# The last MLP's first product as seven block products, in two passes over the features

## The chip, the core and the metric

The kernel runs on one core of one Trainium2 chip. The metric is the device time of one execution in microseconds (us), the median of several runs. The core has five engines with a queue each: TensorE (PE in the profile, its weight loads listed apart as PEld), VectorE (DVE), ScalarE (ACT), GpSimd (POOL) and SyncE (SP), which here issues most of the DMAs. Each engine takes the instructions of its queue in order; between engines they wait on semaphores.

## What is computed

A two-layer encoder trunk for 256 + 1024 = 1280 tokens of 1024 features. Each layer has a mixer and an MLP. The part that matters is the MLP of the second layer, the last step of the kernel:

```python
h = rms_norm(x, norm_mlp[layer, 0])
f = jnp.einsum('bld,df->blf', h, w_ff_in[layer])
f = jnp.einsum('blf,fd->bld', jnp.square(jax.nn.relu(f)), w_ff_out[layer])
x = x + rms_norm(f, norm_mlp[layer, 1])
```

`w_ff_in` is 1024 x 4096, `w_ff_out` 4096 x 1024, all in float32.

## The kernel before

**Products.** A float32 product is made of three matmuls on values split in a high part and a low part: `mm3` (L249 to L256) multiplies high by high, high by low and low by high. `split` (L243 to L247) makes the two parts: a cast on ScalarE (L246) and a subtraction on VectorE (L247). A matmul takes 128 x 128 weights and up to 512 columns of tokens.

**Tokens and features.** The tokens are ten tiles of 128, in two halves of 640 (HT). The 4096 hidden features (DFF) are 32 tiles of 128, or NP = 16 pairs j. The 1024 input features are KT = 8 tiles.

**First product** (`mlp`, from L338; called for the last MLP at L2094). For a feature tile f the weights come in as 512 KB (`w1load`, `raw` in the profile), are split into `w` (three buffers), and then 24 matmuls each (8 tiles k times 3) go over 512 and 256 columns of `xT1` and 512 columns of `xT0`, into PSUM tiles `psi`. `xT0` holds four token tiles that `mixer_out`, the step ahead, has normed and transposed; the other six tiles are normed (`pre_a`) and transposed (`pre_b`, eight transposes into a PSUM tile `pst`, then copies to `xT1`) inside this stage while six feature tiles go over the `xT0` columns ahead. The PSUM pool of `psi` and `pst` has three double banks.

**Between the products.** Each result goes through Relu (L386) and Square (L387) on ScalarE into a staging tile `st`. A pair of feature tiles and two token halves make four blocks of 128 x 640; `sums` (L368 to L376) makes three more by four additions on VectorE, and `store` (L380 to L382) writes all seven, 2240 KB, to DRAM as `hd[j]`.

**Second product** (L436 to the end of `mlp`). It uses seven block products already: with the blocks of `hd[j]` (loads `hr`, split into `hs`) and sums of blocks of `w_ff_out`, seven steps i over 16 pairs k, results in PSUM tiles `po` (L512). 

**What sets the order.** Engines run in program order as the code is written, save that a scheduler may move instructions on a queue when the program is built. SP's queue holds the weight loads, the stores of `hd` and the loads of `hr` in one line. The buffers of the pools, reused in turn, set when a load may start.

Of the kernel before, what the change touches and what calls it, by code (L numbers as in the profile page):

```python
# [13 lines left out]
ALU = mybir.AluOpType  # L14
# [39 lines left out]
def drain(g):  # L54
    for _ in g:
        pass
# [126 lines left out]
class Trunk:  # L183
# [151 lines left out]

    def mlp(self, layer, lay, xT0, g1, side=(), tail=None):  # L338


        side = iter(side)
# [2 lines left out]
        w1, w2 = I["w_ff_in"][layer], I["w_ff_out"][layer]  # L344
        NP = DFF // 256
        with ExitStack() as c:

            cf = ExitStack()
            sp = self.pool(cf, "st", 2, side="right")
            xT1 = self.pool(cf, "xT1", 1, side="right").tile([128, 2, KT, 768], F32R, name="xT1")  # L350
            cx = c.enter_context(ExitStack())
            self.xp = self.pool(cx, "x", 2)
            self.hbp = self.pool(cx, "hb", 2)
            tts = [self.halves[0][4], *self.halves[1]]
            hb = {}

            def norm(i):
                hb[i] = self.pre_a(self.load_x(lay, tts[i]), g1)

            def transpose(i):  # L360
                self.pre_b(hb.pop(i), xT1, (i - 1) % 6 * 128)
            g = pipe(6, norm, lambda i: None, transpose)
            stage = {}

            def w1load(f):
                return self.w8load(w1[:, f * 128:(f + 1) * 128].rearrange("(k p) f -> p k f", p=128), [KT, 128])

            def sums(j):  # L368

                t = stage.pop(j)  # L370
                a11, a21, a12, a22, s1, s2, s4 = (t[:, i] for i in range(7))
                v.tensor_tensor(s1, a21, a22, op=ALU.add)
                v.tensor_tensor(a21, a11, a21, op=ALU.subtract)
                v.tensor_tensor(s2, s1, a11, op=ALU.subtract)
                v.tensor_tensor(s4, a12, s2, op=ALU.subtract)
                stores.append((j, t))  # L376
# [12 lines left out]
            def ffin(f, W, parts):  # L389

                j, z = divmod(f, 2)
                if j not in stage:
                    stage[j] = sp.tile([128, 7, HT], F32, tag="st", name="st")
                d = stage[j][:, 2 * z:2 * z + 2].rearrange("p a t -> p (a t)")
                for o, m, ps in parts:
                    x, i = (xT1, o) if o < 768 else (xT0, o - 768)
                    self.mm3(ps[:, :m], [((W[:, 0, k], W[:, 1, k]), (x[:, 0, k, i:i + m], x[:, 1, k, i:i + m]))
                                         for k in range(KT)])
                    act(ps[:, :m], d[:, o:o + m])

            def banks():
                b = self.bank2([128, 2, 512], "psi")
                return b[:, 0], b[:, 1]

            AHEAD = 6
            jobs = [(f, 0) for f in range(AHEAD)] + [(f, 1) for f in range(AHEAD)] + [(f, None) for f in range(AHEAD, 2 * NP)]
            next(g)
            next(g)
            W = w1load(0)
            odd = None  # L410
            for n, (f, h) in enumerate(jobs):
                parts = []
                if h != 0:
                    b = banks()
                    parts += [(0, 512, b[0]), (512, 256, b[1])]
                if h != 1:
                    if f % 2 == 0:
                        odd = banks()
                    parts.append((768, 512, odd[f % 2]))
                ffin(f, W, parts)  # L420
                if n + 1 < len(jobs):
                    W = w1load(jobs[n + 1][0])
                if h == 0:
                    next(g, None)
                    if f == AHEAD - 1:
                        cx.close()
                        self.cg.close()
                    continue
                if stores:
                    store()  # L430
                if f % 2:
                    sums(f // 2)
                for _ in range(7 if h else 12):
                    next(side, None)
            drain(side)
            cf.close()  # L436
            hp = self.pool(c, "hr", 4)

            ap = [self.pool(c, "am0", 1)]
# [133 lines left out]

            def next2(t):
                self.pre_b(hb.pop(t), nx[0], (t + 4) % 5 * 128)
            sq = {}

            def half(t):
# [45 lines left out]
    class OutProj:  # L624
# [37 lines left out]
        def product(self, i):  # L662
            self.partial(i, self.order)
            del self.M[i]
# [1287 lines left out]
        self.xp = self.pool(c, "x", 2)  # L1952
        self.hbp = self.pool(c, "hb", 2)

    def mixer_out(self, op, layer, head=0):


        I = self.I
        self.gp = self.g1p
        g1 = self.load_gain(I["norm_mlp"][layer, 0:1, :])  # L1960
        xT = self.xtp.tile([128, 2, KT, 512], F32R, tag="xT", name="xT")
        hb = {}
        with ExitStack() as c:
            self.xp = self.pool(c, "x", 2)
# [25 lines left out]

            def finish(i):
                y = op.finish(i, g)
                if i < 4:
                    hb[i] = self.pre_a(y, g1)

            def transpose(i):
                if i < 4:
                    self.pre_b(hb.pop(i), xT, i * 128)

            def product(i):  # L2000
# [7 lines left out]
    def run(self):  # L2008
# [117 lines left out]
```

## Time and profile before

| what | value |
|---|---|
| median of 3 runs | 3134.39 us (3132.23 to 3135.25) |
| the profiled execution, its own time | 3131.81 us |
| its span | 3130.0 us |
| its mean granted TensorE clock | 0.991 |
| TensorE busy | 3031.6 us, 97% of the span |
| weight loads / VectorE / ScalarE / GpSimd busy | 84% / 64% / 40% / 11% |
| DMA | 507.37 MB, mean 162 GB/s |

The span is the time between the first and the last instruction of one execution as the profiler saw it. Times in the rows below are microseconds from the start of that span, unless they are marked as ns. The granted clock is the share of full speed that TensorE was given; 1.00 is 2.4 GHz and 0.50 is 1.2 GHz. The first product of the last MLP runs from about 2282 to 2738 us.

### The profile page before, as it was taken

Reading aid. Unit: us, or ns where it says so; the run is one execution under the profiler, and the core shown is the slowest. Engines: PE = TensorE matmul, PEld = TensorE weight load, DVE = VectorE, ACT = ScalarE, POOL = GpSimd, SP = SyncE. Lnnn points to the kernel's source line nnn. Section 1 sums busy time; section 2 is a strip of 40 time slices with the busy share of each in tenths; the row PEclk is TensorE's granted clock in tenths of the full one; section 3 lists DMA queues with packets and bytes.
Section 4 is the critical chain, followed back from the end, with each engine's and each line's share of the span. In section 5 each row is a group of like instructions: output and inputs, shape, how many; then the busy total and the mean of one; then the engine's idle time right before and its main releaser. Section 6 shows DMA issues by size and latency. Waiting matters only on the chain. (4 is left out here: it accounts for less than half of the span.)

```text
span 3130.0 us, 44212 instructions
## 1 busy us (share of the span) xinstructions
PE 3031.6 (97%) x16768; PEld 2627.5 (84%) x16768; DVE 1998.1 (64%) x3678; ACT 1258.2 (40%) x2269; POOL 329.9 (11%) x555
## 2 busy tenths in 40 slices
PE   8999989999999999999999999997999999999998
PEld 7878878788888788888999899996888888888887
DVE  6688865667767665676865499998542212165765
ACT  5577763444444333354223221112343222243343
POOL 1045640000100000000000223221000000000000
PEclk9999999999999999999999999999999999999999
DMA  4100034456556774676987633324544332464674
GB/s 148 54 13 11 12 104 147 142 187 215 185 168 193 260 225 123 214 229 217 332 312 269 197 116 103 129 86 145 153 149 163 135 133 100 154 218 144 225 233 141
DMA packets 309794, 507.37 MB, mean 162 GB/s; under 512 B 19476, under 2 KB 198646, under 8 KB 297036
## 3 DMA queue, kind: packets, MB, share of 16 engines
q1 hardware_dynamic: 300780, 467.02, 45.5%
q0 software_dynamic: 8800, 37.51, 3.6%
q8 instruction: 132, 2.16, 0.3%
q14 instruction: 82, 0.67, 0.1%
HBM read 340.61 MB, written 163.85 MB: 161 GB/s over the span
## 5 line engine op out<-in xcount | busy, mean ns | idle before, releaser
L255 PE MATMUL psi<-xT,w 128*128 128x512 f32 (+1 forms) x4608 | 915.8, 356 | 6.2 <-DVE xT L247 3.6
L255 PEld LDWEIGHTS psi<-xT,w 128*128 128x128 f32 x4608 | 753.0, 188 | 137.0 <-ACT st L386 14.8
L512 PE MATMUL po<-w,hs 128*128 128x512 f32 x3360 | 777.4, 393 | 4.0 <-ACT hs L246 4.0
L512 PEld LDWEIGHTS po<-w,hs 128*128 128x128 f32 x3360 | 631.6, 189 | 147.6 <-ACT hs L246 4.4
L247 DVE TENSOR_TENSOR w<-raw,w 128x1024 fp32r<-128x1024 f32 (+1 forms) x192 | 182.3, 952 | 351.0 <-ACT w L246 350.7
L247 DVE TENSOR_TENSOR hs<-hr,hs 128x640 fp32r<-128x640 f32 x224 | 183.6, 823 | 239.4 <-ACT hs L246 239.2
L246 ACT CAST hs<-hr 128x640 fp32r<-128x640 f32 x224 | 163.1, 729 | 426.2 <-PE po L512 399.4
L255 PE MATMUL psz<-xT,w 128*128 128x320 f32 (+2 forms) x1920 | 292.2, 311 | 2.6 <-ACT w L246 1.9
L386 ACT ACTIVATE st<-psi 128x512 f32<-128x512 f32 (+1 forms) x192 | 101.0, 526 | 469.8 <-PE psi L255 469.7
L255 PEld LDWEIGHTS psz<-xT,w 128*128 128x128 f32 x1920 | 284.0, 189 | 4.7 <-ACT w L246 2.3
L1048 POOL TENSOR_TENSOR P<-P,sm 128x256 f32<-128x256 f32 x272 | 162.5, 628 | 148.4 <-DVE sm L1045 143.4
L246 ACT CAST w<-raw 128x1024 fp32r<-128x1024 f32 (+1 forms) x192 | 158.9, 829 | 42.4 <-DMA raw<-odd_w_in 13.9
L255 PE MATMUL pso<-wo,M 128*128 128x512 f32 x660 | 159.3, 397 | 8.7 <-ACT M L246 7.1
L255 PEld LDWEIGHTS pso<-wo,M 128*128 128x128 f32 x660 | 124.7, 190 | 38.3 <-ACT M L246 7.3
L1392 PE MATMUL psu<-Z,fb 128*128 128x128 f32 x768 | 100.8, 289 | 19.0 <-DVE t L1731 13.7
L1392 PEld LDWEIGHTS psu<-Z,fb 128*128 128x128 f32 x768 | 95.5, 203 | 23.5 <-issue 16.8
L255 PE MATMUL pss<-kt,qt 128*128 128x512 f32 (+3 forms) x432 | 111.8, 386 | 3.3 <-DVE PT L247 3.0
L387 ACT ACTIVATE st<-st 128x512 f32<-128x512 f32 (+1 forms) x192 | 107.6, 560 | 3.3
L247 DVE TENSOR_TENSOR w<-am,w 128x512 fp32r<-128x512 f32 x128 | 87.0, 684 | 33.3 <-ACT w L246 33.3
L220 POOL DMA_DIRECT2D gain<-norm_mlp x4 | 2.2, 558 | 945.2 <-DVE w L247 926.8
L247 DVE TENSOR_TENSOR PT<-pspt,PT 128x1024 fp32r<-128x1024 f32 (+1 forms) x72 | 83.7, 1163 | 20.0 <-ACT PT L246 19.0
L255 PEld LDWEIGHTS pss<-kt,qt 128*128 128x128 f32 (+1 forms) x432 | 75.6, 189 | 15.9 <-PE pspt L1056 3.6
(341 smaller groups left out, 4160.2 us busy)
## 6 DMA issues: line engine op xcount, KB each, us to landing
hd<-st SPq DMA_DIRECT2D x32, 2240.0 KB
hr<-hd SPq DMA_DIRECT2D x224, 320.0 KB
raw<-w_ff_out SPq DMA_DIRECT2D x112, 512.0 KB
raw<-w_ff_in SPq DMA_DIRECT2D x76, 512.0 KB
x<-xd SPq DMA_DIRECT2D x47, 512.0 KB
wd<-w SPq DMA_DIRECT2D x20, 1024.0 KB
w<-wd POOLq DMA_DIRECT2D x20, 1024.0 KB, 5.4
dec<-c_decay SPq DMA_DIRECT2D x120, 128.0 KB
```

Source lines behind the costliest of these rows:

```text
L220: self.nc.gpsimd.dma_start(g, row.broadcast_to([128, D]))
L246: self.nc.scalar.copy(hi, src)
L247: (eng or self.nc.vector).tensor_tensor(lo, src, hi, op=ALU.subtract)
L255: self.nc.tensor.matmul(out, lhsT=lt[a], rhs=r[b], start=start and i == 0, stop=stop and i == n - 1)
L386: nc.scalar.activation(d, ps, AF.Relu)
L387: nc.scalar.activation(d, d, AF.Square)
L512: nc.tensor.matmul(P[i][t], lhsT=h[:, x, t * 128:(t + 1) * 128], rhs=w[:, y], start=k + n == 0, stop=k == NP - 1 and n == 2)
L1048: nc.gpsimd.tensor_tensor(p, p, sm[:, 2:3].to_broadcast([128, 256]), op=ALU.mult)
L1392: self.nc.tensor.matmul(ps[:, out], lhsT=FB[:, pos, i, out], rhs=z, start=i == 0, stop=i == 1)
```

## The change

The last MLP's first product becomes a product of 2 x 2 blocks as well. The blocks are: input features in two halves of four tiles k, tokens in two halves of 640, the two feature tiles of a pair j. Seven products of 512 x 128 blocks with 512 x 640 blocks take the place of eight. `mlp` gets a flag `blocks`, which is set for the last MLP alone; the first MLP runs the old code, now called `plain`.

Two passes over the 16 pairs:

- Pass 1 makes, for each j, the two products that need no sums of blocks: the weights of the pair's first feature tile by `xT0`, 24 matmuls of 320 columns for each of two column halves, lower four k and upper four k. The first result (p1) is copied from PSUM to `pc`, the second is added to it (`c11`), `c11` goes through Relu and Square, and both, 640 KB, are stored in `hd[j]`. In the same pass the five tiles of the second token half are normed and transposed, and `operands` makes the five right-hand blocks X by six additions and five splits for each tile.
- Pass 2 loads the weights again, as two loads of 512 KB for each j, makes five left-hand operands by four additions and five splits (`wparts`), loads p1 and `c11` back (`prefetch`) and makes the other five products, six additions of 640 columns, three pairs of Relu and Square, and then `sums` and `store` of 2240 KB as before.

`mixer_out` transposes five tiles now (n=5), and `xT0` has 640 columns. The staging tile of pass 2 takes the space of `xT0`. `wslots` moves to a function, and the order of tiles at the end of the MLP is rotated (`rot`).

In the diff lines that are only "..." stand for what is left out; `plain` is the old code, further indented.

```diff
-    def mlp(self, layer, lay, xT0, g1, side=(), tail=None):
+    def mlp(self, layer, lay, xT0, g1, side=(), tail=None, blocks=False):
...
+            def plain():
...
+            def strassen():
+                cf = ExitStack()
+                opp = self.pool(cf, "xo", 1, side="right")
+                X = {q: opp.tile([128, 2, 4, HT], F32R, name=f"xo{q}") for q in (4, 3, 5, 7, 6)}
+                cx = ExitStack()
+                pp = self.pool(cx, "pc", 1)
+                tp = self.pool(cx, "xs", 1)
+                xp = self.pool(cx, "x", 2)
+                xb = {}
+                def norm(i):
+                    x = xb[i] = xp.tile([128, D], F32, tag="x", name="x")
+                    nc.sync.dma_start(x, self.x_src(lay, self.halves[1][i]))
+                    sm = self.small()
+                    self.square_sum(x, sm)
+                    self.root(sm, D)
+                    r = self.rstd(sm, D)
+                    v.scalar_tensor_tensor(x, x, r, g1, op0=ALU.mult, op1=ALU.mult)
+                def operands(i):
+                    x = xb.pop(i)
+                    ps = self.bank2([128, KT, 128], "pst")
+                    for k in range(KT):
+                        nc.tensor.transpose(ps[:, k], x[:, k * 128:(k + 1) * 128], self.ident)
+                    b = tp.tile([128, KT, 128], F32, tag="xb", name="xb")
+                    nc.scalar.copy(b, ps)
+                    b12, b22 = b[:, 0:4], b[:, 4:8]
+                    t = slice(i * 128, (i + 1) * 128)
+                    p = tp.tile([128, 4, 128], F32, tag="xp", name="xp")
+                    q = tp.tile([128, 4, 128], F32, tag="xq", name="xq")
+                    v.tensor_tensor(p, xT0[:, 0, 0:4, t], xT0[:, 1, 0:4, t], op=ALU.add)
+                    v.tensor_tensor(q, b22, b12, op=ALU.subtract)
+                    self.split(X[7][:, :, :, t], q)
+                    v.tensor_tensor(p, b12, p, op=ALU.subtract)
+                    self.split(X[5][:, :, :, t], p)
+                    v.tensor_tensor(q, b22, p, op=ALU.subtract)
+                    self.split(X[6][:, :, :, t], q)
+                    v.tensor_tensor(p, xT0[:, 0, 4:8, t], xT0[:, 1, 4:8, t], op=ALU.add)
+                    self.split(X[3][:, :, :, t], b22)
+                    v.tensor_tensor(p, q, p, op=ALU.subtract)
+                    self.split(X[4][:, :, :, t], p)
+                g = pipe(5, norm, lambda i: None, operands)
+                def product(w, x):
+                    ps = self.bank2([128, 2, 512], "psi")
+                    for c in range(2):
+                        o = slice(c * 320, c * 320 + 320)
+                        self.mm3(ps[:, c, :320], [((w[:, 0, k], w[:, 1, k]), (x[:, 0, k, o], x[:, 1, k, o]))
+                                                  for k in range(4)])
+                    return ps[:, :, :320]
+                def cols(t):
+                    return t.rearrange("p (a t) -> p a t", a=2)
+                next(g)
+                next(g)
+                W = w1load(0)
+                for j in range(NP):
+                    pc = pp.tile([128, 2, HT], F32, tag="pc", name="pc")
+                    p1, c11 = cols(pc[:, 0]), cols(pc[:, 1])
+                    nc.scalar.copy(p1, product(W[:, :, 0:4], xT0[:, :, 0:4]))
+                    ps = product(W[:, :, 4:8], xT0[:, :, 4:8])
+                    if j + 1 < NP:
+                        W = w1load(2 * j + 2)
+                    v.tensor_tensor(c11, p1, ps, op=ALU.add)
+                    act(pc[:, 1], pc[:, 1])
+                    nc.sync.dma_start(self.hd[j][:, 0:2], pc)
+                    if j % 2 == 0:
+                        next(g, None)
+                drain(g)
+                cx.close()
+                self.cg.close()
+                cw = ExitStack()
+                wp = self.pool(cw, "wr", 4)
+                tp = self.pool(cw, "wt", 2)
+                st = self.xtp.tile([128, 2, 7, HT], F32, tag="xT", name="st")
+                ring = wring()
+                raws, parts = {}, []
+                def wload(j):
+                    if j < NP:
+                        raws[j] = [self.raww(w1[z * 512:(z + 1) * 512, j * 256:(j + 1) * 256]
+                                             .rearrange("(k p) f -> p k f", p=128), [4, 256], wp) for z in range(2)]
+                def wparts():
+                    n = 0
+                    for j in range(NP):
+                        lo, hi = raws.pop(j)
+                        a11, a21, a12, a22 = lo[:, :, 0:128], lo[:, :, 128:256], hi[:, :, 0:128], hi[:, :, 128:256]
+                        s3 = tp.tile([128, 4, 128], F32, tag="wt", name="s3")
+                        wload(j + 1)
+                        v.tensor_tensor(s3, a11, a21, op=ALU.subtract)
+                        v.tensor_tensor(a21, a21, a22, op=ALU.add)
+                        v.tensor_tensor(a11, a21, a11, op=ALU.subtract)
+                        for q, src in enumerate((a11, s3, a21, a12, a22)):
+                            if q == 3:
+                                v.tensor_tensor(a12, a12, a11, op=ALU.subtract)
+                            t = ring[n % len(ring)].rearrange("p (a k f) -> p a k f", a=2, k=4)
+                            n += 1
+                            self.split(t, src)
+                            parts.append(t)
+                            yield
+                wgen = wparts()
+                def prefetch(j):
+                    if j < NP:
+                        stage[j] = st[:, j % 2]
+                        nc.sync.dma_start(stage[j][:, 0:2], self.hd[j][:, 0:2])
+                wload(0)
+                prefetch(0)
+                for _ in range(4):
+                    next(wgen)
+                for j in range(NP):
+                    t = stage[j]
+                    u, c22, c21 = cols(t[:, 0]), cols(t[:, 2]), cols(t[:, 3])
+                    for q in (6, 7, 5, 3, 4):
+                        ps = product(parts.pop(0), X[q])
+                        next(wgen, None)
+                        if q == 6:
+                            v.tensor_tensor(u, u, ps, op=ALU.add)
+                            if j:
+                                sums(j - 1)
+                        elif q == 7:
+                            v.tensor_tensor(c21, u, ps, op=ALU.add)
+                        elif q == 5:
+                            v.tensor_tensor(c22, c21, ps, op=ALU.add)
+                            v.tensor_tensor(u, u, ps, op=ALU.add)
+                            act(t[:, 2], t[:, 2])
+                            if j:
+                                store()
+                        elif q == 3:
+                            v.tensor_tensor(u, u, ps, op=ALU.add)
+                            act(t[:, 0], t[:, 0])
+                            prefetch(j + 1)
+                        else:
+                            v.tensor_tensor(c21, c21, ps, op=ALU.subtract)
+                            act(t[:, 3], t[:, 3])
+                sums(NP - 1)
+                cw.close()
+                cf.close()
+            def wring():
+                return [t[:, i * 1024:(i + 1) * 1024] for t in [self.w8.tile([128, 2048], F32R, tag="w8", name="w4")
+                                                                for _ in range(self.nw8)] for i in range(2)]
+            (strassen if blocks else plain)()
...
-            wslots = [t[:, i * 1024:(i + 1) * 1024] for t in [self.w8.tile([128, 2048], F32R, tag="w8", name="w4")
-                                                              for _ in range(self.nw8)] for i in range(2)]
+            wslots = wring()
...
+            rot = 0 if blocks else 4
...
-                tt = self.halves[0][(t + 4) % 5]
+                tt = self.halves[0][(t + rot) % 5]
...
-    def mixer_out(self, op, layer, head=0):
+    def mixer_out(self, op, layer, head=0, n=4):
...
-        xT = self.xtp.tile([128, 2, KT, 512], F32R, tag="xT", name="xT")
+        xT = self.xtp.tile([128, 2, KT, n * 128], F32R, tag="xT", name="xT")
...
-                if i < 4:
+                if i < n:
...
-            xT, g1 = self.mixer_out(op, 1)
+            xT, g1 = self.mixer_out(op, 1, n=5)
...
-            self.mlp(1, 3, xT, g1)
+            self.mlp(1, 3, xT, g1, blocks=True)
```

**The order of instructions.** Three places, as the built programs have them.

ScalarE in the first product, before, one feature tile. `st<-psi` is Relu and `st<-st` Square; `w<-raw` is the high part of the next tile's weights:

```order
L386 ACTIVATE st<-psi 128x512
L246 CAST w<-raw 128x1024
L387 ACTIVATE st<-st 128x512
L386 ACTIVATE st<-psi 128x512
L387 ACTIVATE st<-st 128x512
L386 ACTIVATE st<-psi 128x256
L387 ACTIVATE st<-st 128x256
```

Here the cast of the weights stands among the activations of one tile.

ScalarE in pass 1, after, around the copy of a transposed tile (`xb<-pst`). `xo` are the parts of X, `xq` and `xp` the sums they are made of, `pc<-psi` the copy of p1:

```order
L246 CAST w<-raw 128x1024
L472 COPY xb<-pst 128x1024
L506 COPY pc<-psi 128x640
L246 CAST xo_21062<-xb 128x4x128
L246 CAST xo_21064<-xq 128x4x128
L373 ACTIVATE pc<-pc 128x640
L246 CAST xo_21063<-xp 128x4x128
L374 ACTIVATE pc<-pc 128x640
```

The cast of the weights now stands ahead of the copy that frees the PSUM banks of the transposes, and the copy of p1 behind it.

SP in the first product, before (`hd_111` is `hd[3]`):

```order
L382 DMA hd_111<-st 128x4480
L470 DMA hr<-hd_111 128x640
L260 DMA raw<-w_ff_in 128x8x128 x2
L382 DMA hd_112<-st 128x4480
L470 DMA hr<-hd_112 128x640
L260 DMA raw<-w_ff_in 128x8x128 x2
```

For each pair there are one store, one load for the second product and two weight loads.

SP at the change of passes, after (`hd_108` is `hd[0]`, `hd_123` is `hd[15]`; `raw` of 128x4x256 are weight loads of pass 2):

```order
L512 DMA hd_120<-pc 128x1280
L512 DMA hd_121<-pc 128x1280
L512 DMA hd_122<-pc 128x1280
L555 DMA st<-hd_108 128x1280
L555 DMA st<-hd_109 128x1280
L512 DMA hd_123<-pc 128x1280
L260 DMA raw<-w_ff_in 128x4x256 x8
L369 DMA hd_108<-st 128x4480
L260 DMA raw<-w_ff_in 128x4x256 x2
L555 DMA st<-hd_110 128x1280
```

The loads of half results for the first two pairs have moved ahead of the last store of pass 1, and the first weight loads of pass 2 stand behind it. From then on a round has one store, two weight loads and one load of half results.

## Rows read from the trace of the kernel before

**Rows 1.** The page's chain of work that ended last, by line.

```profile
PE psi L255 14%; PE po L512 12%; PE pso L255 3%; PE psz L255 3%; PE psu L1392 2%; PE pe L1739 1%; PE po L1739 1%; DVE t L1729 0%; PE pe L1741 0%; PE po L1741 0%; POOL Y L1732 0%; PE psu L1838 0%; POOL Y L1733 0%; PE psya L1739 0%; DMA w<-wd 0%
```

**Rows 2.** Windows: us, busy of PE, PEld, DVE, ACT, POOL, PEclk, DMA share, GB/s.

```profile
2324.00:2737.60 413.60, 413.60 (x2161) 350.06 (x2160) 91.69 (x102) 127.72 (x220) 0.00 (x0) 1.00 0.38 136
```

**Rows 3.** Timeline of PE: start, us, engine, line, operation, out<-in, count.

```profile
2281.87 5.65 PE L255 MATMUL psi<-xT,w 128*128 128x512 f32 x24
...
2296.19 5.72 PE L255 MATMUL psi<-xT,w 128*128 128x512 f32 x24
2301.75 1.03 PE L297 MATMUL pst<-ident,hb 128*128 128x128 f32 x8
2302.60 5.76 PE L255 MATMUL psi<-xT,w 128*128 128x512 f32 x24
...
2737.60 22.60 PE L512 MATMUL po<-w,hs 128*128 128x512 f32 x99
```

**Rows 4.** Timeline of PE and PEld in the Hyena input product.

```profile
1545.76 7.15 PEld L255 LDWEIGHTS psz<-xT,w 128*128 128x128 f32 x48
1545.78 7.39 PE L255 MATMUL psz<-xT,w 128*128 128x320 f32 x48
1553.01 1.89 PE L1469 MATMUL pss<-zp,fa 128*128 128x256 f32 x8
```

**Rows 5.** Groups by line and shape, first product: busy, mean ns, idle before.

```profile
L255 PEld LDWEIGHTS psi<-xT,w 128*128 128x128 f32 x2302 | 376.4, 188 | 72.2 <-ACT st L386 7.3 <-DVE xT L247 2.0
L247 DVE TENSOR_TENSOR w<-raw,w 128x1024 fp32r<-128x1024 f32 x35 | 42.9, 1226 | 290.3 <-ACT w L246 290.3
...
L246 ACT CAST w<-raw 128x1024 fp32r<-128x1024 f32 x35 | 36.5, 1042 | 2.9 <-PE psi L255 2.9
...
L372 DVE TENSOR_TENSOR st<-st 128x640 f32<-128x640 f32 x15 | 12.3, 819 | 0.0
...
L246 ACT CAST xT<-pst 128x1024 fp32r<-128x1024 f32 x6 | 6.0, 1011 | 0.0
```

**Rows 6.** Groups by line and shape from 2200 to the end.

```profile
L246 ACT CAST hs<-hr 128x640 fp32r<-128x640 f32 x112 | 81.8, 730 | 217.7 <-PE po L512 202.6 <-issue 10.8 <-DMA hr<-hd 4.1
...
L247 DVE TENSOR_TENSOR w<-am,w 128x512 fp32r<-128x512 f32 x64 | 43.7, 685 | 32.0 <-ACT w L246 32.0
...
L246 ACT CAST w<-am 128x512 fp32r<-128x512 f32 x64 | 39.4, 616 | 0.0
```

**Rows 7.** The tile psz, ScalarE's copy: least, median, greatest ns.

```profile
L1540 ACT COPY zs<-psz x20: 692/692/699, 1477.5 to 1689.3; 128x640 f32<-128x640 f32 x20
```

**Rows 8.** Timeline of SP's DMA issues and of the first reader.

```profile
2241.07 0.37 SPq L260 DMA_DIRECT2D raw<-w_ff_in  x1
...
2245.01 1.05 ACT L246 CAST w<-raw 128x1024 fp32r<-128x1024 f32 x1 [5.28 <-DMA raw<-w_ff_in]
...
2342.26 0.34 SPq L382 DMA_DIRECT2D hd<-st  x1
...
2349.14 0.34 SPq L470 DMA_DIRECT2D hr<-hd  x1
...
2408.71 0.34 SPq L382 DMA_DIRECT2D hd<-st  x1
2417.35 0.34 SPq L470 DMA_DIRECT2D hr<-hd  x1
...
2420.17 0.73 ACT L246 CAST hs<-hr 128x640 fp32r<-128x640 f32 x1 [1.49 <-DMA hr<-hd]
```

**Rows 9.** Timeline of PE around an idle stretch in the mixer.

```profile
2153.97 0.73 PE L255 MATMUL pso<-xT,M 128*128 128x512 f32 x2 [1.33 <-ACT M L246]
2162.42 5.26 PE L255 MATMUL pso<-xT,M 128*128 128x512 f32 x13 [7.73 <-DVE M L247]
2167.52 0.63 PE L255 MATMUL pso<-wo,M 128*128 128x512 f32 x2
```

**Rows 10.** The window behind that stretch, columns as in rows 2.

```profile
2160.00:2165.00 5.00, 2.58 (x6) 2.09 (x7) 5.00 (x14) 1.05 (x1) 0.00 (x0) 0.50 0.55 216
```

More of the change, by code (lines that the diff above doesn't have):

```diff
@@ L346, in mlp @@
         with ExitStack() as c:
[L348 to L362, printed above, removed]
             stage = {}
@@ L387, in act @@
                 nc.scalar.activation(d, d, AF.Square)
[L389 to L434, printed above, removed]
@@ L435, in mlp, with transpose, ffin, banks @@
-            drain(side)
-            cf.close()
+            def plain():
+                cf = ExitStack()
+                sp = self.pool(cf, "st", 2, side="right")
+                xT1 = self.pool(cf, "xT1", 1, side="right").tile([128, 2, KT, 768], F32R, name="xT1")
+                cx = c.enter_context(ExitStack())
+                self.xp = self.pool(cx, "x", 2)
+                self.hbp = self.pool(cx, "hb", 2)
+                tts = [self.halves[0][4], *self.halves[1]]
+                hb = {}
+                def norm(i):
+                    hb[i] = self.pre_a(self.load_x(lay, tts[i]), g1)
+                def transpose(i):
+                    self.pre_b(hb.pop(i), xT1, (i - 1) % 6 * 128)
+                g = pipe(6, norm, lambda i: None, transpose)
+                def ffin(f, W, parts):
+                    j, z = divmod(f, 2)
+                    if j not in stage:
+                        stage[j] = sp.tile([128, 7, HT], F32, tag="st", name="st")
+                    d = stage[j][:, 2 * z:2 * z + 2].rearrange("p a t -> p (a t)")
+                    for o, m, ps in parts:
+                        x, i = (xT1, o) if o < 768 else (xT0, o - 768)
+                        self.mm3(ps[:, :m], [((W[:, 0, k], W[:, 1, k]), (x[:, 0, k, i:i + m], x[:, 1, k, i:i + m]))
+                                             for k in range(KT)])
+                        act(ps[:, :m], d[:, o:o + m])
+                def banks():
+                    b = self.bank2([128, 2, 512], "psi")
+                    return b[:, 0], b[:, 1]
+                AHEAD = 6
+                jobs = [(f, 0) for f in range(AHEAD)] + [(f, 1) for f in range(AHEAD)] + [(f, None) for f in range(AHEAD, 2 * NP)]
+                next(g)
+                next(g)
+                W = w1load(0)
+                odd = None
+                for n, (f, h) in enumerate(jobs):
+                    parts = []
+                    if h != 0:
+                        b = banks()
+                        parts += [(0, 512, b[0]), (512, 256, b[1])]
+                    if h != 1:
+                        if f % 2 == 0:
+                            odd = banks()
+                        parts.append((768, 512, odd[f % 2]))
+                    ffin(f, W, parts)
+                    if n + 1 < len(jobs):
+                        W = w1load(jobs[n + 1][0])
+                    if h == 0:
+                        next(g, None)
+                        if f == AHEAD - 1:
+                            cx.close()
+                            self.cg.close()
+                        continue
+                    if stores:
+                        store()
+                    if f % 2:
+                        sums(f // 2)
+                    for _ in range(7 if h else 12):
+                        next(side, None)
+                drain(side)
+                cf.close()
@@ new lines, in strassen, with norm @@
+            def strassen():
+                cf = ExitStack()
+                opp = self.pool(cf, "xo", 1, side="right")
[5 more added lines that the diff above has]
+                xb = {}
+                def norm(i):
+                    x = xb[i] = xp.tile([128, D], F32, tag="x", name="x")
[37 more added lines that the diff above has]
+                    return t.rearrange("p (a t) -> p a t", a=2)
+                next(g)
+                next(g)
+                W = w1load(0)
+                for j in range(NP):
[9 more added lines that the diff above has]
+                    if j % 2 == 0:
+                        next(g, None)
+                drain(g)
+                cx.close()
+                self.cg.close()
+                cw = ExitStack()
[52 more added lines that the diff above has]
+                            if j:
+                                store()
+                        elif q == 3:
[7 more added lines that the diff above has]
+                cw.close()
+                cf.close()
@@ L574, in next2 @@
             def next2(t):
-                self.pre_b(hb.pop(t), nx[0], (t + 4) % 5 * 128)
+                self.pre_b(hb.pop(t), nx[0], (t + rot) % 5 * 128)
             sq = {}
@@ L1992, in finish @@
                 y = op.finish(i, g)
-                if i < 4:
+                if i < n:
                     hb[i] = self.pre_a(y, g1)
             def transpose(i):
-                if i < 4:
+                if i < n:
                     self.pre_b(hb.pop(i), xT, i * 128)
```

## The prediction

> **What bounds the kernel now.** I read the chain of work that ended last first. It is TensorE almost throughout, and the line `psi L255`, the first products of the two MLPs, has the largest share, 14% of the span [rows 1]. The table by windows then tells whether the stage that is rewritten waits for anything: from 2324.00 to the first `po` matmul TensorE is busy 413.60 of 413.60 us at granted clock 1.00, VectorE 91.69, ScalarE 127.72, and the DMA engines .38 of the time at 136 GB/s [rows 2]. So this stage is bound by matmul columns, and there is room on the other engines. Its length is read from TensorE's timeline: first `psi` at 2281.87, first `po` at 2737.60, that is **455.73 us** [rows 3]. The change must be priced in matmuls first, then in whatever interrupts them.
>
> **The price of a matmul.** A 512-column one: 24 in 2301.75 - 2296.19 = 5.56 us, 0.232 each [rows 3]. The new ones have 320 columns, a width which this stage does not have but the Hyena input product has: 48 of them from 1545.78 until the next operation at 1553.01, 7.23 us, **0.1506** each [rows 4]. That is the same mm3 helper with weights changed for every matmul.
>
> The Trainium skill (TensorE: Matmul & The Clock Gate, Back-to-back issue gap) gives N/2.4 + 2.5 ns for a warm gap, which is 135.8 ns at 320 columns. By it the products of the new stage would take 365.1 us instead of the 404.8 below. This trace disagrees: it shows 150.6 ns at 320 and 232 ns at 512, where the rule says 215.8, so the measurement decides.
>
> **Part by part.** (a) Products: 16 pairs x 7 products x 24 = 2688 matmuls of 320 columns, in place of 2304 of 512, 256 and 512. 2688 x 0.1506 = **404.8 us**.
>
> (b) Transposes: five tiles instead of six stay in the stage. Eight cost 2302.60 - 2301.75 = 0.85 with the hand-over [rows 3]; I take 0.82, together **4.1**. The sixth moves into mixer_out with all its instructions, where TensorE is the engine in line as well: 0.8 there, not in the stage.
>
> (c) Pass 1, beside the products. In ScalarE's new queue a cast of W stands ahead of the copy `xb`, and that cast cannot start before the product in front of the transposes has ended, because it writes that product's weight buffer. The product behind the transposes takes the PSUM bank that they wrote. So it waits for cast 1.04 + copy 1.01 [rows 5] less the transposes 0.82, plus two or three hand-overs of some 0.06 to 0.1: 1.4 us, four times, and about 0.5 for the first tile: **6**. Below it could be 2 (where the cast finds its buffer free), above 10 (where the `pc` copy, 0.69 [rows 7], stands in between as well). The rest of the new work lies beside matmuls. Per two pairs VectorE has 2 low halves of W at 1.226, 2 `c11` at 0.82, and for a tile six adds and five low halves at 0.685 [rows 5, 6]: 4.1 + 7.5 = 11.6 of some 16.7 us, without the norm. ScalarE has 2 x (1.04 + 0.69 + 0.73 + 0.73), the copy 1.01 and five casts at 0.616: 10.5. Neither is the bound.
>
> (d) The change of passes. Pass 2 needs its weight operands. Their buffers lie in space that pass 1 gives up, and their loads stand on SP behind the last 640 KB store of `pc`. After the last product of pass 1: `c11` 0.82, Relu and Square 0.73 each like the 128x640 cast [rows 6] = 2.3; the copy of p1 comes some 1.0 late behind the store before, since there is one `pc`; two SP issues 0.34 + 0.37 = 0.7; the 512 KB load lands in 2245.01 - 2241.07 = 3.94 [rows 8] and shares the DMA engines with the store ahead. A store of 2240 KB lands in 6.88 and a load of 320 KB in 2.82 [rows 8]; from these 2.11 us per 1000 KB, so 1.35 of transfer for 640 KB, together with some queueing 1.9, so 5.8. Then two adds 1.37 and a cast 0.62, and the low half for the second of the three matmuls, of which 0.5 shows. 2.3 + 1.0 + 0.7 + 5.8 + 2.0 + 0.5 = **12.3** of an idle TensorE. Bounds 9 (no lateness, no sharing) and 16 (a slow store and both halves awaited).
>
> (e) The clock after that gap. No gap stands in the stage of before, but one of 7.73 us is elsewhere [rows 9]: the window 2160 to 2165 has granted clock 0.50, the lower of the two levels (1.2 GHz), and 13 512-column matmuls take 2167.52 - 2162.42 = 5.10 us [rows 9, 10] where 13 x 0.232 = 3.0. Hence **2.1**, between 0 and 4 because the new gap is longer.
>
> (f) Pass 2 into the second product: the last combinations and the first `hs` casts come after the last `psi`. 0 to 3, I take **0.9**; before has next to nothing there.
>
> Costed at nothing in pass 2: per pair VectorE has 4 adds and 5 low halves at 0.685, six combinations and four `sums` at 0.82, 14.4 us; ScalarE five casts and three pairs of activations, 7.5; a round of 120 matmuls lasts 18.07. If that cover went, VectorE would be the next bound, only 3.7 us below. DMA moves 1024 + 640 + 2240 KB a round, about 220 GB/s, as much as the trace's 216 GB/s at a share of .55 [rows 10].
>
> **The sum.** 404.8 + 4.1 + 6 + 12.3 + 2.1 + 0.9 = 430.2, against 455.73: 25.5 less, of which 0.8 goes to mixer_out. **24.7 us** saved. The profiled execution took 3131.81, so 3107.1 for one like it; it is 2.58 below the median of the runs, so 3134.39 - 24.7 = **3109.7**. With all low ends (2, 9, 0, 0) the stage is 419.9, with all high ends (10, 16, 4, 3) 441.9: the forecast's own range is 3099 to 3121.
>
> **Rivals.** Cheap change of passes: the weight loads get ahead, or the engines overlap better, and the gap is 4 us or less. Then (d) and (e) fall to about 5, saving 34, 3100. Against it speaks the SP order. Chance .10.
>
> Pass 1 turns into a store loop. One `pc`: the next p1 copy waits for the store to land. Copy 0.69 + `c11` 0.82 + activations 1.46 + landing must fit into 7.23; it decides at a landing of 4.2 us. The rows give 3.5 for 640 KB by interpolation, but with a 512 KB weight load ahead about 5.0, that is 8.0 a round, 0.8 x 15 = 12, less some 2 that the PSUM banks absorb: 3120. At a landing of 5.9 the saving is gone, 3135. Chance .15.
>
> Slower: pass 2 turns into a loop through DRAM. The two halves of `st` must be stored before the next half results are loaded into them. In a round the first `u` add releases `sums`; four of them and it are 4.1, the store lands after x, issues take 0.7, the 640 KB load 3.9 with what runs beside it, and only then can the `u` add of the next round start. A round is at least 8.7 + x; x is 6.88 to 8.64 in the rows [rows 8], where the loop just fits into 18.07. From x = 9.4 it sets the pace; banks absorb about 4 us once; from x = 11.4 it has eaten the gain, and x = 12.5, a store that shares with two weight loads and the load of half results, costs 14 x 3.1 - 4 = 39, so 3149. For it speaks that these transfers do come together, against it that 1.0 to 2.5 us are to spare and that the DMA load is moderate. Chance .08.
>
> The edit does not do what it says: fewer columns, yet no less time, since the matmuls are shorter than their weight loads, which last 188 ns in the mean in this stage [rows 5]. A pitch of 0.160 in place of 0.1506 would take all of the saving: 2688 x 0.0094 = 25, so 3134. Against it, 48 loads go by in 7.15 us, 149 ns each, in the 320-column product [rows 4]. Chance .05.
>
> **How the numbers follow.** The forecast has .62. Faster by over 0.2% (6.3 us, about what a measurement of this kernel can tell from no change) holds the forecast, the cheap change of passes and .11 of the store loop: .83. Within it are .03 of the store loop and the .05 of the pitch: .08. Slower are the loop through DRAM and the store loop's last .01: .09. Range 3097 to 3127: from the cheap change of passes to the milder store loop, with all bounds of the forecast.
>
> **What would show it.** In the profile of the changed kernel: `psi` groups of 48 in 7.2 us (a); TensorE idle for ScalarE behind each group of `pst`, 1.1 to 2 us (c); one idle stretch of 9 to 16 us about 140 us after the first `psi`, followed by matmuls at clock 0.50 (d, e); no idle of TensorE for VectorE inside pass 2. A store loop shows as waits ended by the DMA of `pc` in every round of pass 1, the loop through DRAM as rounds longer than 18.1 us, with the `u` add waiting for its load. The prediction is wrong if pass 2's rounds differ from 18.1, or if the idle stretch is not between 9 and 16.

## The result, and the profile after

The changed kernel took **3101.49 us** in the median of 4 runs (3097.91 to 3102.89), the kernel before 3134.82 (3132.23 to 3135.92): a ratio of 0.9893, with a 95% interval from 0.9876 to 0.991, so 33.3 us less, with 28 to 39 in the interval. The forecast was 3109.7, 24.7 us less. The profiled execution of the changed kernel has a span of 3101.1 us.

The stage from the first `psi` to the first `po` is where it comes from. The timeline of TensorE, which answers to [rows 3] (start, busy us, operation, count, idle time ahead and what ended it):

```profile
2284.87 7.20 PE L255 MATMUL psi<-xT,w 128*128 128x320 f32 x48
2292.93 1.06 PE L470 MATMUL pst<-ident,x 128*128 128x128 f32 x8 [0.86 <-DVE sm L237]
2293.75 14.33 PE L255 MATMUL psi<-xT,w 128*128 128x320 f32 x96
...
2324.49 1.04 PE L470 MATMUL pst<-ident,x 128*128 128x128 f32 x8
2326.70 14.34 PE L255 MATMUL psi<-xT,w 128*128 128x320 f32 x96 [1.17 <-ACT xb L472]
...
2359.48 49.54 PE L255 MATMUL psi<-xT,w 128*128 128x320 f32 x336 [1.17 <-ACT xb L472]
...
2422.44 1.44 PE L255 MATMUL psi<-xo,w 128*128 128x320 f32 x4 [13.43 <-ACT w L246]
2424.67 282.94 PE L255 MATMUL psi<-xo,w 128*128 128x320 f32 x1916 [0.79 <-DVE w L247]
2707.51 1.19 PE L667 MATMUL po<-w,hs 128*128 128x512 f32 x4
```

Pass 1 runs to about 2409.0, then TensorE stands idle for 13.43 us, and pass 2 is one unbroken group of 1916. From 2284.87 to 2707.51 it is **422.64 us**, against 455.73: 33.1 less. The rest of the two profiles differs by 4 us the other way. 3 of them stand ahead of the stage, and they do not come from the changed part: the two profiles are 3.1 us apart already at 617 us, long before its first instruction.

The windows behind the idle stretch and of the rest of pass 2 (columns as in [rows 2]):

```profile
2422.00:2427.00 5.00, 3.77 (x13) 3.37 (x14) 4.28 (x7) 2.05 (x4) 0.00 (x0) 0.50 0.13 28
2427.00:2432.00 5.00, 5.00 (x31) 5.00 (x31) 4.17 (x8) 1.25 (x2) 0.00 (x0) 0.86 0.61 195
...
2450.00:2700.00 250.00, 250.00 (x1707) 250.00 (x1706) 182.43 (x264) 105.04 (x154) 0.00 (x0) 1.00 0.64 231
```

The clock falls to 0.50 (1.2 GHz) behind the idle stretch, as in [rows 9, 10]. From 2450 to 2700 TensorE is busy 250.00 of 250.00 us while VectorE's load has grown to 73% of the time; before it was 22% [rows 2].

### The profile page after: what moved, and what is told of

It is laid out like the page before. It is cut to its first block, busy times and chain, and to the rows that moved or that the text cites. A ratio compares the mean times of both kernels' runs of the same rounds, so it can differ in the third digit from the quotient of the medians.

```text
span 3101.1 us, 45562 instructions
## 1 busy us (share of the span) xinstructions
PE 2982.7 (96%) x17152; PEld 2646.4 (85%) x17152; DVE 2169.4 (70%) x3962; ACT 1304.3 (42%) x2304; POOL 329.3 (11%) x555
## 3 DMA queue, kind: packets, MB, share of 16 engines
q8 instruction: 135, 2.21, 0.3%
## 5 line engine op out<-in xcount | busy, mean ns | idle before, releaser
L255 PE MATMUL psi<-xT,w 128*128 128x512 f32 (+2 forms) x3072 | 581.9, 344 | 8.6 <-ACT xb L472 3.5
L255 PEld LDWEIGHTS psi<-xT,w 128*128 128x128 f32 x3072 | 488.9, 189 | 70.8 <-ACT st L373 7.5
L247 DVE TENSOR_TENSOR hs<-hr,hs 128x640 fp32r<-128x640 f32 x224 | 183.5, 823 | 223.4 <-ACT hs L246 223.1
L255 PE MATMUL psi<-xo,w 128*128 128x320 f32 x1920 | 284.4, 310 | 14.2 <-ACT w L246 13.4
L255 PEld LDWEIGHTS psi<-xo,w 128*128 128x128 f32 x1920 | 283.7, 189 | 14.9 <-ACT w L246 13.7
L247 DVE TENSOR_TENSOR w<-raw,w 128x512 fp32r<-128x512 f32 (+1 forms) x234 | 199.1, 855 | 90.4 <-ACT w L246 90.0
L246 ACT CAST w<-raw 128x512 fp32r<-128x512 f32 (+1 forms) x234 | 175.5, 752 | 172.0 <-PE psi L255 126.9
L373 ACT ACTIVATE st<-psi 128x512 f32<-128x512 f32 (+1 forms) x96 | 50.4, 525 | 179.2 <-PE psi L255 179.1
L1549 PE MATMUL psu<-Z,fb 128*128 128x128 f32 x768 | 101.8, 292 | 18.1 <-DVE t L1888 14.0
L247 DVE TENSOR_TENSOR PT<-pspt,PT 128x1024 fp32r<-128x1024 f32 (+1 forms) x72 | 83.7, 1163 | 19.9 <-ACT PT L246 18.9
L374 ACT ACTIVATE st<-st 128x512 f32<-128x512 f32 (+2 forms) x144 | 89.2, 619 | 2.9
```

The source lines that it names most:

```text
L246: self.nc.scalar.copy(hi, src)
L247: (eng or self.nc.vector).tensor_tensor(lo, src, hi, op=ALU.subtract)
L255: self.nc.tensor.matmul(out, lhsT=lt[a], rhs=r[b], start=start and i == 0, stop=stop and i == n - 1)
L1549: self.nc.tensor.matmul(ps[:, out], lhsT=FB[:, pos, i, out], rhs=z, start=i == 0, stop=i == 1)
```

## Where the matmul price of the prediction came from

The prediction divided 7.23 us by the 48 matmuls of a group [rows 4]. The timeline of the kernel before, asked for windows that begin at the last `pss` ahead of that group and inside the group, tells it otherwise:

```profile
1545.75 0.38 PE L1469 MATMUL pss<-zp,fa 128*128 128x256 f32 x1
...
1546.12 7.06 PE L255 MATMUL psz<-xT,w 128*128 128x320 f32 x47
1553.01 0.59 PE L1469 MATMUL pss<-zp,fa 128*128 128x256 f32 x2
```

Without its first matmul the group has 47 in 6.89 us, 0.1466 each. The first one alone stands from 1545.78 to 1546.12, 0.34. It begins 0.03 behind the start of the last `pss` (1545.75), while the `pss` ahead of that one start 0.22 apart. So some 0.19 us of the group's 7.23 are still time of the last `pss`, and 2688/48 = 56 times that is 10 us. In the changed kernel pass 2 has no such change of operation inside it.

## The experiments

Times against the changed kernel are against its second measurement, 3099.46 us; where a range is given, its other end is against the first, 3101.49.

**The changed kernel again** (e0).

> The changed kernel once more, beside the edits, as their base. In its first profile TensorE ran through the 2688 block matmuls at 0.1467 us each, stood idle 13.43 + 0.79 us at the change of passes, and 4.88 us behind the transposes of pass 1. Theory (these three terms make the stage of 422.6 us): the same idle stretches again within 0.5 us and a time of 3098 to 3103. If the idle stretches vary by microseconds from one execution to the next, their cause is not the order of instructions.

3099.46 us (3096.21 to 3100.91). The waits behind the transposes were 0.85 and three of 1.17 us, the gap 13.76 us, the stage 423.09. So these stretches belong to the order of instructions and not to one execution. Pass 2 was not free of waits this time: TensorE waited twice for VectorE's `u` add, 0.23 and 0.33 us.

**Weight loads of pass 2 early** (e1). Its core, with `pc` moved to the other side of SBUF to make room:

```diff
+                    if j == 9:
+                        drain(g)
+                        cx.close()
+                        self.cg.close()
+                        wp, tp = self.pool(cw, "wr", 4), self.pool(cw, "wt", 2)
+                        wload(0)
+                        wload(1)
```

> The first two pairs of weight loads of pass 2 get buffers of their own from pair 9 of pass 1 on, so that they no longer stand behind the last store; the adds and splits of the first operands move ahead of the end of pass 1 with them. Theory A (the gap of 14.2 us is the landing of the loads plus the making of the first operand, and the low clock behind it costs 2 us more): the gap goes below 1 us, no matmul runs at clock 0.50 there, and the time falls by 14 to 17 us against the changed kernel, to about 3086. Rival B (something else holds pass 2, for instance the loads of half results or st, whose space is that of xT0): the gap stays over 3.5 us and the gain is below 11 us.

3085.13 us, 14.3 less; ratio to the kernel before 0.9846 (0.9831 to 0.9861). Its timeline of TensorE at the change of passes:

```profile
2357.95 49.54 PE L255 MATMUL psi<-xT,w 128*128 128x320 f32 x336 [1.17 <-ACT xb L472]
2407.33 282.18 PE L255 MATMUL psi<-xo,w 128*128 128x320 f32 x1920
2689.40 1.21 PE L672 MATMUL po<-w,hs 128*128 128x512 f32 x4
```

There is no idle time left between the passes, and 1920 matmuls take 282.07 us, 0.1469 each, without a slow start: the gap was the loads and the making of operands, as theory A says. The half results and `st` held nothing. The adds and splits moved ahead with the loads, although the code asks for them at the end of pass 1 as before: the order on a queue is that of the built program.

**Early loads alone** (e1b). The operands are held behind the last `c11`:

```diff
-                for _ in range(4):
-                    next(wgen)
+                with self.tc.issue_after(last.ins):
+                    for _ in range(4):
+                        next(wgen)
```

> The same early loads, but the adds and splits of the first four operands are held behind the last c11 of pass 1. Theory A: the landing is off the path, the making of the operand stays: c11 0.82, three adds and one low half that stand ahead of the first cast in VectorE's queue (4 x 0.69 = 2.8, or 4.8 where the second pair's adds stand between too), cast 0.62, low half 0.69: a gap of 5 to 8 us, and a time between the changed kernel and the kernel with early operands, 8 to 10 us below the changed one. Rival B (the landing was hidden anyway): a gap of 12 us or more.

3089.97 us, 9.5 less. The gap:

```profile
2409.41 284.15 PE L255 MATMUL psi<-xo,w 128*128 128x320 f32 x1920 [4.63 <-ACT w L246]
```

4.63 us in place of 13.43, and no second wait, a little below the 5 to 8 expected: the way to the loaded weights (activations, store, issue, landing) had cost about 9 us, `c11` and the making of the operand 4.6. Its 1920 matmuls take 284.05 us, 2.0 more than in e1, and the granted clock is 0.50 in the first 4.6 us behind the gap: here a gap of 4.6 us brings the slow clock as one of 14 us does.

**Two buffers for p1** (e3).

```diff
-                    b = tp.tile([128, KT, 128], F32, tag="xb", name="xb")
+                    b = x.rearrange("p (k t) -> p k t", k=KT)
...
-                    pc = pp.tile([128, 2, HT], F32, tag="pc", name="pc")
-                    p1, c11 = cols(pc[:, 0]), cols(pc[:, 1])
+                    pa = pp.tile([128, HT], F32, tag="pa", name="pa", bufs=2)
+                    pc = pp.tile([128, HT], F32, tag="pc", name="pc")
+                    p1, c11 = cols(pa), cols(pc)
```

> p1 of pass 1 gets two buffers in place of one (c11 apart from it in one, the transposed tile is copied back over x to make room, two stores of 320 KB in place of one of 640 KB). Theory C (the PSUM banks behind the transposes are held because the copy of p1 waits for the store of the pair before, with one buffer): the waits of 1.17 to 1.37 us behind four of the five groups of transposes shrink below 0.3, together 4 us, time about 3097. Rival D (the prediction's step: the wait is the cast of W and the copy xb ahead, whatever the buffer of p1): the waits stay at 1.1 to 1.4 and the time stays within 1.5 us of the changed kernel.

3092.67 us, 6.8 less, more than the 4 that theory C gave. ScalarE's timeline around a group of transposes, first of the changed kernel, where TensorE ended a pair at 2340.88 and waited until 2343.09:

```profile
2341.08 1.05 ACT L246 CAST w<-raw 128x1024 fp32r<-128x1024 f32 x1 [1.26 <-PE psi L255]
2342.03 1.00 ACT L472 COPY xb<-pst 128x1024 f32<-128x1024 f32 x1
...
2343.59 0.69 ACT L506 COPY pc<-psi 128x640 f32<-128x640 f32 x1
```

The copy of p1 (L506) is that of the pair that had ended, and comes 2.7 us behind the pair's end. So by this order the banks of that pair were still taken, and the first to come free was that of the transposes. Then of e3, ScalarE and TensorE:

```profile
2332.34 0.67 ACT L507 COPY pa<-psi 128x640 f32<-128x640 f32 x1
...
2337.39 0.99 ACT L472 COPY x<-pst 128x1024 f32<-128x1024 f32 x1
```

```profile
2333.69 1.03 PE L470 MATMUL pst<-ident,x 128*128 128x128 f32 x8
2334.48 14.32 PE L255 MATMUL psi<-xT,w 128*128 128x320 f32 x96
```

Here the copy of p1 ends before the transposes begin, the copy of the transposed tile is 3.7 us behind them, later than in the changed kernel, and TensorE does not wait. Rival D, the prediction's step, falls. From the transposes to the next product it is 0.79 us now where it was 2.21, so a group cost 1.4 us and not the 1.17 of the wait alone; four groups make 5.9 of the gain, the shorter gap of 12.80 us most of the rest. The edit also splits the store in two and copies the transposed tile back over `x`; these were not tried apart, and which bank a product takes is not in the profile, so the way by the banks is read from the order of the copies.

**Half results stored twice** (e6).

```diff
+                    nc.sync.dma_start(hd2[j % 2], pc)
                     nc.sync.dma_start(self.hd[j][:, 0:2], pc)
```

> Pass 1 of the changed kernel writes each 640 KB of pc a second time, ahead of the store proper. Theory (store loop of one pc buffer): copy 0.69, c11 0.82, activations 1.48, issue 0.35 and landing 3.03 are 6.4 us of a pair's 7.05; with 1.4 us of transfer and an issue more it is 8.1, so each of the 16 pairs is 1.0 us longer, some 13 to 16 us in all, less what the banks take up. Rival (the three banks and the early weights hide it, since TensorE waits for no store there): within 2 us of the changed kernel.

3115.2 us (two runs), 14 to 16 more than the changed kernel. ScalarE and TensorE in the second part of pass 1:

```profile
2374.11 0.69 ACT L508 COPY pc<-psi 128x640 f32<-128x640 f32 x1 [2.22 <-DMA hd<-pc]
...
2381.87 0.69 ACT L508 COPY pc<-psi 128x640 f32<-128x640 f32 x1 [2.13 <-DMA hd<-pc]
```

```profile
2374.86 7.31 PE L255 MATMUL psi<-xT,w 128*128 128x320 f32 x48 [0.53 <-ACT pc L508]
2382.61 7.31 PE L255 MATMUL psi<-xT,w 128*128 128x320 f32 x48 [0.45 <-ACT pc L508]
```

A pair takes 7.75 us now, less than the 8.1 expected, and is paced by the store: the loop is real. In the changed kernel the last copy of p1 is

```profile
2407.86 0.70 ACT L506 COPY pc<-psi 128x640 f32<-128x640 f32 x1 [3.05 <-DMA hd<-pc]
```

It waits 3.05 us for the store and begins 6.14 us behind the copy before it (2401.72), which also waited for its store. That is below the 7.05 of a pair's matmuls: the loop just fitted.

**Staging tiles stored twice** (e5).

```diff
                             if j:
+                                nc.sync.dma_start(hd2[j % 2], stores[0][1])
                                 store()
```

> Pass 2 of the changed kernel writes each 2240 KB staging tile a second time, to a scratch tensor and ahead of the store proper. Theory E (the loop through DRAM of the prediction: add, sums, store, load, add): a round lasts at least 8.7 us plus the landing of the store; in the changed kernel that is 8.7 + 7.8 = 16.5, below the 17.6 of the matmuls. With 4.7 to 6.9 us more of landing it is 21 to 23.4, so 14 rounds cost 48 to 81 us more. Rival F (there is no such loop, only the DMA engines' rate): 6.3 MB a round at the 340 GB/s of the densest stretches are 18.4 us, at most 12 us more in all.

3127.52 us, 26 to 28 more; neither number. A round of e5 is 19.21 us:

```profile
2549.05 17.84 PE L255 MATMUL psi<-xo,w 128*128 128x320 f32 x120 [1.37 <-DVE st L568]
2568.27 17.84 PE L255 MATMUL psi<-xo,w 128*128 128x320 f32 x120 [1.37 <-DVE st L568]
```

```profile
2562.98 0.42 SPq L369 DMA_DIRECT2D hd<-st  x1
2564.64 9.26 SPq L260 DMA_DIRECT2D raw<-w_ff_in  x2
2575.97 0.34 SPq L556 DMA_DIRECT2D st<-hd  x1
```

```profile
2577.98 0.83 DVE L359 TENSOR_TENSOR st<-st 128x640 f32<-128x640 f32 x1 [0.97 <-ACT st L374]
...
2583.13 0.69 DVE L247 TENSOR_TENSOR w<-raw,w 128x512 fp32r<-128x512 f32 x1 [1.39 <-ACT w L246]
...
2586.52 0.81 DVE L568 TENSOR_TENSOR st<-st,psi 128x640 f32<-128x640 f32 x1
```

The store lands 12.99 us after its issue (7.97 in the changed kernel), so the formula wants 8.7 + 13.0 = 21.7. It fails because `sums` (from L359) ran 8.5 us ahead of the `u` add (L568) of the same round: they do not wait for it, although the code names them after it. TensorE waits 1.37 us a round for that add, which stands in VectorE's queue behind the sums and the adds for later operands and shows no wait for a DMA of its own. The DMA engines were busy .87 of the time at 330 GB/s in these rounds. One chain without a DMA fills the round: the cast at 2582.48 waits for a product to end, 14.2 us into the round; the low half (L247) waits for that cast, four adds and the `u` add follow, and TensorE goes on at 2587.48, 19.2 us after 2568.27. In the changed kernel the `u` add stands among the four `sums` and not behind these adds, so the edit changed the order on VectorE's queue too, and is no clean test of the store alone. What sets the 19.21 was not tried apart; it stays open. That this edit costs 26 to 28 us and not 48 to 81 is what is shown.

**Products twice** (e7).

```diff
-                    for c in range(2):
+                    for c in [0, 1] * times:
...
-                        ps = product(parts.pop(0), X[q])
+                        ps = product(parts.pop(0), X[q], 2)
```

> Each of the 80 products of pass 2 is made twice into the same bank (the second starts the sum anew), 3840 more matmuls of 320 columns and nothing else. Theory (a matmul costs what the starts inside a long group show, 0.1467 us): 563 us more. Rival (the prediction's 0.1506, read from groups of 48): 578 us more.

The expectation miscounts: a product has 24 matmuls, so the edit adds 80 x 24 = 1920, for which the two prices give 281.7 and 289.2 us. Measured 3384.63 us, 283.1 to 285.2 more. The timeline tells it more sharply:

```profile
2422.05 564.17 PE L255 MATMUL psi<-xo,w 128*128 128x320 f32 x3836 [0.45 <-DVE w L247]
2986.06 1.09 PE L667 MATMUL po<-w,hs 128*128 128x512 f32 x4
```

564.01 us here against 282.84 in the changed kernel: 281.2 for 1920 more, **0.1464** each. The price inside a group holds.

**Both edits together** (e4, e8, e11). The first pair's loads early, two buffers for p1.

> Two buffers for p1, and the weight loads of pass 2's first pair early (its second pair's follow at the change of passes). The two edits took 6.8 and 14.3 us each. Theory (two waits in different places, which add up): no idle of TensorE over 0.9 us in the stage, 400 to 402 us from the first psi to the first po, time 3077 to 3081. Rival (the second pair's late loads turn into a wait of their own inside pass 2): an idle stretch of 2 us or more some 16 to 20 us behind the change of passes, time 3083 or more.

3085.94 us, no better than e1 alone. Not pass 2 but the start was in the way:

```profile
2296.50 1.94 PE L470 MATMUL pst<-ident,x 128*128 128x128 f32 x8 [6.60 <-DVE sm L236]
2298.09 15.32 PE L255 MATMUL psi<-xT,w 128*128 128x320 f32 x96
```

The load of the first `x` tile was issued 5.15 us behind the first `psi`, where it was 0.2 in the changed kernel: by the layout the tile now lay where `mixer_out` keeps an `x` until its last addition. The attempt to load it into the other buffer:

```diff
+                xp.tile([128, D], F32, tag="x", name="x")
```

> The kernel with both edits, save that the first token tile of pass 1 is loaded into the other of the two x buffers, whose space does not have to wait for the last norm of mixer_out. In the kernel with both edits that wait held the first transposes back by 6.60 us and let the clock fall behind them. Theory: the wait shrinks to the 0.8 to 1.0 us of the other kernels, the stage from the first psi to the first po is 2688 x 0.1467 + 5 x 0.8 + 0.9 = 399 to 401 us, and the time 3077 to 3080. Rival (the two edits' gains overlap, or the unchanged part of the kernel takes some of them back): 3082 or more.

3084.89 us, and the wait was 6.48. The first load was again issued 5.15 us behind the first `psi`, so the edit did not move it; that a tile which is never written takes no space would explain this, but was not tried by itself. With the space laid out anew (buffers of the weight loads below, used as scratch of the sums until then, `x` above):

```diff
-                tp = self.pool(cx, "xs", 1)
+                cw = ExitStack()
+                wps = {0: self.pool(cw, "wr", 2)}
                 xp = self.pool(cx, "x", 2)
```

> Both edits once more, with the SBUF space laid out anew: the buffers of the early weight loads lie where mixer_out had its own x tiles and serve as scratch of the sums until then, and the x tiles of pass 1 lie above, as in the changed kernel, so that their loads need not wait for mixer_out's last addition. In the two kernels before, those loads were issued at 2287.85 and 2291.09, 5.15 us behind the first psi, and held the first transposes back by 6.5 us. Theory: the wait shrinks to 0.8 to 1.0 us, the stage from the first psi to the first po is 399 to 401 us, and the time 3076 to 3080. Rival (what is gained in the stage is lost elsewhere): the stage is as short but the time 3082 or more.

```profile
2283.71 7.20 PE L255 MATMUL psi<-xT,w 128*128 128x320 f32 x48
2292.34 1.06 PE L471 MATMUL pst<-ident,x 128*128 128x128 f32 x8 [1.43 <-DVE sm L237]
...
2402.32 281.77 PE L255 MATMUL psi<-xo,w 128*128 128x320 f32 x1920
2683.99 1.19 PE L675 MATMUL po<-w,hs 128*128 128x512 f32 x4
```

**3079.72 us** (3077.6 to 3080.5), ratio 0.9824 (0.9811 to 0.9838): 55 us below the kernel before and 20 to 22 below the changed one. The stage is 400.28 us and waits only for the first norm, 1.43 us in place of the 0.8 to 1.0 expected; 2688 x 0.1468 and five groups of transposes of 0.8 are 398.6 of it. So the two gains do add up once the space is laid out for both.

## Why the prediction was right, and where it was off

The direction, the mechanism (TensorE's columns are the bound, the other engines and the DMA cover the new work) and the list of what interrupts them held. The forecast came out 8.2 us too slow, and the steps say why.

- **(a) Products: the term that was mis-sized.** 2688 x 0.1468 = 394.6 us, not 404.8: 10.2 us, more than the whole error. The row was the right operation at the right width, but it held 0.19 us of the operation ahead, and the group was too short to divide by its count. With it the prediction's round of pass 2, 18.1 us, falls too: 120 matmuls take 17.6, so by the prediction's own sign ("wrong if pass 2's rounds differ from 18.1") this step failed. The rule of the Trainium skill (TensorE: Matmul & The Clock Gate, Back-to-back issue gap), by estimate 135.8 ns at 320 columns, stands 11 ns below what these groups show; that section gives it for an isolated matmul, not for a stream with a weight load for each.
- **(b)** 4.1 expected; from each group of transposes to the next product, less the waits, 0.8 to 1.0, so 5.0.
- **(c)** 6 expected; 0.86 + 1.37 + 3 x 1.17 = 5.7. The number was right, the cause only half, and that is luck. The rows do show TensorE released by the copy `xb` behind the cast, as the prediction had it, behind three of the four groups; behind the other (1.37) it is the copy of p1. But e3 shows that the wait hangs on the single buffer of p1: with two buffers `xb` comes later still and TensorE does not wait.
- **(d)** 12.3 expected; 13.43 + 0.79 = 14.2. The copy of p1 held nothing up at the end (-1.0). The issue and the landing of the loads were 0.4 and 6.5, together close to the 6.5 expected. The making of the operand was 4.1 + 0.8, not 2.5: three adds and a low half stand in VectorE's queue ahead of the cast that TensorE waits for, and the prediction had counted two adds.
- **(e)** 2.1 expected. The first four matmuls were busy for 1.44 in place of some 0.75, the other 1916 were 1.4 over 1916 x 0.1469: 2.1.
- **(f)** 0.9 expected; 0.56, four matmuls behind the first `po`, so just outside the 422.64.

The measured terms (a) to (e) are 394.6 + 5.0 + 5.7 + 14.2 + 2.1 = 421.6 of the 422.64 us.

The measured time fell close to the 3100 of the first rival, but not by its mechanism: that asked for a gap of 4 us or less. Of the other rivals the store loop of pass 1 did not come about, with a wait of 3.05 us for the store where a landing of 4.2 decides, and e6 shows the loop itself. The loop through DRAM did not either, and its formula does not hold (e5). The matmuls were not held by their weight loads.

## What to carry to other kernels

Price a matmul from the starts inside a long group, or from the difference of two groups: the length of a short group can hold time of the operation before it, and dividing by its count multiplies that into every matmul of the new stage. At a change of phase ask which loads stand behind the last store on the queue and whether their space is free earlier; space freed a few rounds ahead was worth 14 us here, 9.5 of them for the loads alone; the whole change had brought 33. A wait named after one engine's copy can be the fault of a buffer elsewhere: give the suspect a second buffer and see which waits go.

## What the runs showed of the hardware

- Matmuls of 320 columns follow each other at 0.1464 to 0.1469 us at clock 1.00 with new weights for each one, whether the DMA engines move 394 GB/s, as beside the group at 1546, or 231:

```profile
1546.00:1553.00 7.00, 7.00 (x49) 7.00 (x48) 6.79 (x15) 0.59 (x1) 0.00 (x0) 1.00 1.04 394
```

- At the change of passes the low clock costs about the same behind a gap of 4.6 us (2.0 us, e1b) as behind one of 14.2 us (2.1 us). Behind gaps of one length it need not: with e4's gap of 6.60 us the transposes and the 96 matmuls behind it took 0.8 and 1.0 us longer than in e11, with e8's of 6.48 us 0.8 and 2.0 (granted clock 0.57 from 2296 to 2301 in e4, 0.50 from 2299 to 2304 in e8).
